# A two-layer hybrid decoder on one core: z's tiles in the form of the conv tiles, weight splits shared out anew between engines, one product for the mask of a head pair

## Chip, cores and metric

The kernel runs on one core of one Trainium2 chip. The metric is the device time of the program in microseconds (us). PE is TensorE's matmul stream, PEld its weight loads, DVE is VectorE, ACT is ScalarE, POOL is GpSimd, SP is SyncE, which issues most DMA transfers here.

## What is computed

A trunk of two layers over 256 tokens of width 1024, all in float32. From the reference, cut:

```python
mix = W_out( sigmoid(g_att) * P_att(MoBA(x)) + sigmoid(g_ssm) * P_ssm(Mamba2SSD(x)) )
h   = LayerNorm(ALPHA * x + mix)
x   = LayerNorm(ALPHA * h + W_down(relu(W_up h)^2))
...
q, k, v, z, xbc, dt_raw, g_att, g_ssm = _split(x @ w_in, IN_SPLITS)   # 1024 x3, 2048, 4096, 32, 1024 x2
...
xbc = jax.nn.silu(causal_dwconv(xbc, conv_w, conv_b))                 # 4 taps; xs 2048, B 1024, C 1024
dt = jax.nn.softplus(dt_raw + dt_bias)
a = -jnp.exp(a_log)
xdt = xs * dt[..., None]                                              # 32 heads of 64
decay = jnp.where(causal, jnp.exp(a_cs[..., :, None] - a_cs[..., None, :]), 0.0)   # a_cs = cumsum(dt * a)
y = einsum((C B^T of the head's group) * decay, xdt) + xs * d_skip    # 8 groups of 4 heads
hf = y * jax.nn.silu(z)
hf = hf * lax.rsqrt(mean over each group of hf^2 + RMS_EPS) * ssm_norm_w
```

The chunk of the state-space part is the whole sequence, so there is no carried state. The attention has 16 heads of 64 and one block, so it is plain causal attention.

## The kernel before

**Products.** Every large product multiplies x by weights in float32. Both are split into two parts: a high part, rounded by a cast to the type fp32r, and a low part, the difference. Three products of parts are added: high x high, high weight x low x, low weight x high x. `X[2*L]` holds x as `[128, 8, 2, 256]`: for each of eight k blocks of 128 channels the 256 tokens of the high part, and beside them the 256 of the low part. `gemm_ct` (L440) makes a tile of 128 output channels by 256 tokens with 24 matmuls of 256 columns (L446 to L448). `gemm_ct2` (L450), which the conv tiles use, runs the high weight over both parts of x in one matmul of 512 columns (`both`, L460), and the low weight over the high part in one of 256 columns (`left`, L467). Its output takes 512 columns of PSUM, a whole bank; the right half is then added to the left (`take_right`, a copy on ACT, L474; `add_left`, an addition on DVE, L477).

**Weights.** The weights come in 185 halves for each layer, of 128 x 1024 numbers each, in the order of use. A half is loaded by a DMA on SP (`load_half`, L129), its high part `whi` is cast on ACT (`high_half`, L136), its low part `wlo` is subtracted on DVE, or on GpSimd where `aside(h)` says so (`low_half`, L144):

```python
    def aside(h):

        return 5 <= h < 37 and h % 2
...
    def need(L, h, s, early=None):
        low = s - LOW_AHEAD if early is None else early
        lows[low].append((L, h))
        highs[low - 2].append((L, h))
        loads[low - 2 - LOAD_AHEAD].append((L, h))
```

Half 4 holds dt, halves 5 to 36 the 32 conv tiles, 37 to 56 q, k and v, 57 to 72 the 16 tiles of z, 73 to 88 the two gates.

**The order.** It is written out by hand in slots, 370 for each layer; `B` is the layer's first slot. A slot holds a piece of TensorE's large products (four k blocks of a tile in conv and z), and what `at(slot, function)` puts there on any engine. For each slot the program issues, in this order, the high casts, the low subtractions, the steps, the loads, and the slot's matmuls. A half is loaded fourteen slots ahead of its first matmul, cast six and subtracted four slots ahead. Every engine works off its own instructions in program order and waits on semaphores for its inputs.

**Stages.** In layer 0, in us of the profiled execution: the first q tiles to 22, dt 22 to 25, conv 25 to 126, q, k and v 126 to 195, z 195 to 255, gates 255 to 309, attention projection 309 to 333, state-space projection 333 to 377, output projection 377 to 400, the MLP 400 to 570. Layer 1 follows in the same order. The state-space and attention work of DVE, ACT and small matmuls runs beside the conv stage's end, q, k, v, z, and the gates: four heads of a group g at a time, a pair p of heads in one tile `E[p]` of 128 x 2 x 384 (`ss_exp`, then `ss_mask`, L823, then `ss_y`, L834).

**Around the change.** dt's product is evacuated by ACT into `dtc` (L487), transposed on TensorE (L492), and `dt_softplus` (L503 to L522) makes dt from it on DVE: seventeen small steps that wait on each other, with one Exp on ACT inside, all issued at slot B+13. Ahead of them on DVE, in layer 0, stand the steps that reduce the rope angles (L302 to L322). Each conv tile has three taps on DVE (L583), which read PSUM, and one on ACT. `z` and the gates are evacuated by `act_evac` and `gate_evac`, which apply Silu and Sigmoid on ACT as they read PSUM. ACT applies one function table at a time; a change of table is a table load of its own. Powers of the norms are the only GpSimd work in z's stage (L354, at 128 x 8).

## Time and profile before

| | us |
|---|---|
| median of 3 runs (range) | 1156.51 (1156.08 to 1157.07) |
| profiled execution, its own time | 1155.81 |
| its span | 1153.7 |
| PE busy | 1137.2 |
| DVE busy | 887.5 |
| ACT busy | 672.0 |
| POOL busy | 133.4 |

The span is the stretch from the first to the last instruction that the profiler recorded; the time of the execution holds 2.1 us more. The busy times are of that one execution. The granted clock of TensorE shows 9 in all forty slices of the page, nine tenths or more of full speed throughout.

### The profile page before, as it was taken

The numbers are of one execution on the slowest core, as the hardware profiler recorded it, in microseconds if no ns is written. First come the engines' busy times: TensorE is split into PE (matmuls) and PEld (weight loads), VectorE is DVE, ScalarE is ACT, GpSimd is POOL, SyncE is SP. The second block draws the span as 40 slices with busy tenths as digits, with TensorE's granted clock in tenths as the row PEclk, the third lists the DMA queues.
The fourth block names the chain that finished last, engine by engine and source line by source line (L and its number), as shares of the span: only waits on it lengthen the run. The fifth ranks groups of instructions, "written<-read, shape, count | busy, mean of one in ns | idle before, by whom it ended". The sixth has DMA issues, their size and how long they took to land.

```text
span 1153.7 us, 16860 instructions
## 1 busy us (share of the span) xinstructions
PE 1137.2 (99%) x6282; PEld 958.5 (83%) x6282; DVE 887.5 (77%) x1619; ACT 672.0 (58%) x1016; POOL 133.4 (12%) x99
## 2 busy tenths in 40 slices
PE   8999999999999999999999999999999999999997
PEld 5788888997888888888888888888878888888885
DVE  5899987899965884665779999778998569566565
ACT  5677755888743353453457776568887353444441
POOL 3344000011110000000033420000110100000001
PEclk9999999999999999999999999999999999999999
DMA  8545565545477456557444556645446655556630
GB/s 304 213 163 181 172 186 165 174 138 192 148 256 267 169 167 203 183 171 270 156 152 167 167 179 190 193 147 165 139 156 199 222 216 206 186 192 199 213 135 36
DMA packets 61392, 211.65 MB, mean 183 GB/s; under 512 B 7008, under 2 KB 7360, under 8 KB 61312
## 3 DMA queue, kind: packets, MB, share of 16 engines
q1 hardware_dynamic: 59696, 205.88, 53.7%
q0 software_dynamic: 1472, 4.46, 1.4%
q8 instruction: 49, 0.80, 0.3%
q14 instruction: 31, 0.25, 0.1%
q10 hardware_dynamic: 144, 0.26, 0.1%
HBM read 209.45 MB, written 1.11 MB: 183 GB/s over the span
## 4 chain that ended last, share of the span: by engine, by line
PE 92%; DVE 4%; DMA 1%; ACT 1%; issue 1%; SPq 0%; POOL 0%; DVEq 0%; POOLq 0%; ACTq 0%
PE up L460 9%; PE acc_x L460 8%; PE acc_d L154 5%; PE acc_d L156 5%; PE acc_d L155 5%; PE up L467 5%; PE acc_x L467 4%; PE acc_z L446 3%; PE acc_z L447 3%; PE acc_z L448 3%; PE yp L834 2%; PE sp L722 1%; PE av L765 1%; DMA raw<-in_w_dram 1%; DVE wlo L144 1%; PE acc_sp01b L171 1%
## 5 line engine op out<-in xcount | busy, mean ns | idle before, releaser
L144 DVE TENSOR_TENSOR wlo<-raw,whi 128x1024 fp32r<-128x1024 f32 (+1 forms) x341 | 428.2, 1272 | 25.7 <-ACT whi L136 7.8
L136 ACT CAST whi<-raw 128x1024 fp32r<-128x1024 f32 (+1 forms) x373 | 380.2, 1044 | 46.8 <-DVE wlo L144 17.1
L460 PE MATMUL acc_x<-x,whi 128*128 128x512 f32 x512 | 132.7, 395 | 0.0
L460 PE MATMUL up<-x,whi 128*128 128x512 f32 x448 | 114.9, 392 | 0.0
L477 DVE TENSOR_TENSOR rl<-up,rl 128x256 f32<-128x256 f32 x56 | 23.8, 425 | 117.0 <-ACT rl L474 117.0
L474 ACT COPY rl<-up 128x256 f32<-128x256 f32 x56 | 20.9, 373 | 142.4 <-PE up L460 142.4
L460 PEld LDWEIGHTS acc_x<-x,whi 128*128 128x128 f32 x512 | 90.7, 189 | 15.0
L583 DVE SCALAR_TENSOR_TENSOR cv<-acc_x,pc,cv 128x253 f32<-128x253 f32 (+2 forms) x192 | 91.9, 479 | 4.5
L144 POOL TENSOR_TENSOR wlo<-raw,whi 128x1024 fp32r<-128x1024 f32 x32 | 80.1, 2504 | 124.0 <-ACT whi L136 93.2
L460 PEld LDWEIGHTS up<-x,whi 128*128 128x128 f32 x448 | 80.4, 189 | 14.0
L467 PEld LDWEIGHTS acc_x<-x,wlo 128*128 128x128 f32 x512 | 70.6, 190 | 8.1 <-DVE wlo L144 2.5
L467 PE MATMUL acc_x<-x,wlo 128*128 128x256 f32 x512 | 75.3, 285 | 2.1 <-DVE wlo L144 2.1
L354 POOL TENSOR_TENSOR rc<-rc,mhalf 128x8 f32<-128x8 f32 x16 | 28.9, 1803 | 406.1 <-DVE nm L742 238.3
L446 PE MATMUL acc_z<-x,whi 128*128 128x256 f32 x256 | 74.7, 292 | 0.0
L447 PE MATMUL acc_z<-x,whi 128*128 128x256 f32 x256 | 72.3, 283 | 0.0
L448 PE MATMUL acc_z<-x,wlo 128*128 128x256 f32 x256 | 72.3, 282 | 0.0
L467 PEld LDWEIGHTS up<-x,wlo 128*128 128x128 f32 x448 | 61.2, 190 | 4.4
L467 PE MATMUL up<-x,wlo 128*128 128x256 f32 x448 | 62.9, 283 | 0.0
L579 ACT ACTIVATE cv<-acc_x,pc 128x256 f32<-128x256 f32 x64 | 36.8, 574 | 44.3 <-DVE acc_x L477 44.3
L446 PEld LDWEIGHTS acc_z<-x,whi 128*128 128x128 f32 x256 | 48.7, 190 | 3.4 <-issue 3.3
L447 PEld LDWEIGHTS acc_z<-x,whi 128*128 128x128 f32 x256 | 48.9, 191 | 0.1
L448 PEld LDWEIGHTS acc_z<-x,wlo 128*128 128x128 f32 x256 | 48.8, 190 | 0.0
(964 smaller groups left out, 2405.1 us busy)
## 6 DMA issues: line engine op xcount, KB each, us to landing
raw<-in_w_dram SPq DMA_DIRECT2D x370, 512.0 KB, 4.1
pb<-csd SPq DMA_DIRECT2D x32, 256.0 KB, 3.9
ln<-in_lnp_dram POOLq DMA_DIRECT2D x16, 256.0 KB, 6.4
x_tok<-in_x_dram SPq DMA_DIRECT2D x1, 1024.0 KB, 8.5
xraw<-in_xT_dram SPq DMA_DIRECT2D x3, 256.0 KB, 7.3
...
```

Source lines behind the costliest of these rows:

```text
L136: nc.scalar.copy(out=W[key][:, c], in_=raws[key][:, c])
L144: eng.tensor_tensor(out=lo[:, c], in0=raw[:, c], in1=W[key][:, c].bitcast(F32), op=OP.subtract)
L154: nc.tensor.matmul(o, xh, wh, start=first, stop=False)
L155: nc.tensor.matmul(o, xh, wl, start=False, stop=False)
L156: nc.tensor.matmul(o, xl, wh, start=False, stop=last)
L446: nc.tensor.matmul(o, a, xh[:, kk, :], start=(k == 0), stop=False)
L447: nc.tensor.matmul(o, a, xl[:, kk, :], start=False, stop=False)
L448: nc.tensor.matmul(o, b, xh[:, kk, :], start=False, stop=(k == KD - 1))
L460: nc.tensor.matmul(o, wh[:, (4 * half + i) * 128:(4 * half + i) * 128 + 128], x2[:, kk].rearrange("p j s -> p (j s)"), start=(k0 + i == 0) ...
L467: nc.tensor.matmul(o[:, 0:S], wl[:, (4 * half + i) * 128:(4 * half + i) * 128 + 128], x2[:, kk, 0, :], start=False, stop=False)
L579: nc.scalar.activation(c, o, AF.Identity, scale=pc[:, q + 3:q + 4], bias=pc[:, q + 4:q + 5])
L583: nc.vector.scalar_tensor_tensor(out=c[:, d:S], in0=o[:, 0:S - d], scalar=pc[:, q + j:q + j + 1], in1=c[:, d:S], op0=OP.mult, op1=OP.add)
```

## The change

- z uses `gemm_ct2`: 8 matmuls of 512 and 8 of 256 columns for a tile. Each of the 16 tiles of a layer has a bank of its own, a right copy on ACT and a left addition on DVE; Silu then works in SBUF on two or four tiles at once.
- In the conv stage GpSimd makes the low part of the halves that 3 does not divide (21 a layer instead of 16). In z's stage it makes the low parts of the odd halves 57 to 71 and, new, the high casts of the even halves 58 to 72.
- The mask of a head pair is one product of `E[p]` with the group's masked C B^T; the factor dt is taken out of it and multiplied into the turned xs by GpSimd (`xs_dt`, two products of 128 x 512 for each of four blocks).
- The gates are copied out of PSUM by ACT, and the four sigmoids of a layer run on SBUF tiles at slots 180 and 181, behind the last attention Exp. ACT's table loads fall from 42 to 34.
- Both Exp of an attention head pair stand in one slot, both normalisations in the next; the steps of the state-space norm move by a slot or some.

```diff
     def aside(h):

-        return 5 <= h < 37 and h % 2
+        return 5 <= h < 37 and h % 3 or 57 <= h < 73 and h % 2
+    CAST_ASIDE = range(58, 73, 2)
...
         for c in pieces(key, only):
-            nc.scalar.copy(out=W[key][:, c], in_=raws[key][:, c])
+            copy = nc.gpsimd.tensor_copy if h in CAST_ASIDE else nc.scalar.copy
+            copy(out=W[key][:, c], in_=raws[key][:, c])
...
+        def xs_dt(b, t):
+            x = xs_t[b][:, t, :].rearrange("p (h d) -> p h d", h=8)
+            nc.gpsimd.tensor_tensor(out=x, in0=x, in1=P["dt"][:, t, 8 * b:8 * b + 8].unsqueeze(2).to_broadcast(
+                [128, 8, 64]), op=OP.mult)
...
-                    at(res(r + 12 + j), xs_turn, b, j)
+                    e = res(r + 12 + j)
+                    at(e, xs_turn, b, j)
+                    at(e, xs_dt, b, j)
...
-            for j in range(2):
-                nc.scalar.activation(d[b][:, 2 * j:2 * j + 2, :].rearrange("p k s -> p (k s)"), banks[j]["o"], func)
-
-        for b in range(4):
-            banks = [ct_bank(B + 114, 57, 4 * b + 2 * j, 4 * b + 2 * j + 2, "z") for j in range(2)]
-            at(B + 114 + 8 * b + 8, act_evac, zs, b, banks, AF.Silu, "z")
+        def z_slot(i, half):
+            if half == 0:
+                zb[i] = new_acc(f"acc_z{L}_{i}")
+            gemm_ct2(zb[i], 57 + i, half, lambda k: (X[2 * L][2], k))
+
+        def z_right(i):
+            if i % 4 == 0:
+                zs[i // 4] = u_tile(f"z{L}{i // 4}", shape=(128, 4, S))
+            take_right(zs[i // 4][:, i % 4, :], zb[i])
+
+        def z_left(i):
+            add_left(zs[i // 4][:, i % 4, :], zb.pop(i))
+
+        def z_silu(b, r=slice(0, 4)):
+            nc.scalar.activation(zs[b][:, r, :], zs[b][:, r, :], AF.Silu)
+
+        for i in range(16):
+            base = B + 114 + 2 * i
+            need(L, 57 + i, base)
+            for half in range(2):
+                slots[base + half] = (z_slot, i, half)
+            at(base + 2, z_right, i)
+            at(base + 3, z_left, i)
+            if i in (1, 3):
+                at(base + 4, z_silu, 0, slice(i - 1, i + 1))
+            elif i % 4 == 3:
+                at(base + 6, z_silu, i // 4)
...
             for t in range(2):
-                nc.scalar.activation(d[n][:, t, :], f.tile[t], AF.Sigmoid)
+                nc.scalar.copy(out=d[n][:, t, :], in_=f.tile[t])
+
+        def gate_sigmoid(d, n):
+            nc.scalar.activation(d[n], d[n], AF.Sigmoid)
...
+                at(B + GATES + n, gate_sigmoid, d, n)
...
             for i in range(2):
-                at(s + 1 + i, at_exp, 2 * p + i)
-                at(s + 2 + i, at_norm, 2 * p + i)
+                at(s + 1, at_exp, 2 * p + i)
+            for i in range(2):
+                at(s + 2, at_norm, 2 * p + i)
...
         def ss_mask(p):
-            e, dt, cb = E[p], P["dt"], cbm[p // 2]
-            for i in range(2):
-                h = 2 * p + i
-                for t in range(2):
-                    r = slice(256 * t, 256 + 128 * t)
-                    nc.vector.scalar_tensor_tensor(out=e[:, i, r], in0=e[:, i, r], scalar=dt[:, t, h:h + 1],
-                                                   in1=cb[:, r], op0=OP.mult, op1=OP.mult)
+            e = E[p]
+            nc.vector.tensor_tensor(out=e, in0=e, in1=cbm[p // 2].unsqueeze(1).to_broadcast([128, 2, 384]),
+                                    op=OP.mult)
...
-            s = free = max(v + 2, B + 114 + 8 * (g // 2) + 10, free + 7)
-            for i, step in ((-1, ss_gate), (1, ss_square), (2, ss_add), (3, ss_sq_high), (5, ss_sq_low)):
+            s = free = max(v + 2, B + 114 + (4 * g + 8 if g < 2 else 8 * (g // 2) + 13), free + 7)
+            for i, step in ((-1, ss_gate), (1, ss_square), (2, ss_add), (5, ss_sq_high), (6, ss_sq_low)):
```

**GpSimd at the head of the conv stage.** In the order rows a tile's name carries its half and a running number: `wlo_8_336` is the low part of half 8. GpSimd's first subtractions of layer 0, before:

```order
L144 TENSOR_TENSOR wlo_5_239<-raw_5_135,whi_5_219 128x1024
L144 TENSOR_TENSOR wlo_7_304<-raw_7_159,whi_7_261 128x1024
L144 TENSOR_TENSOR wlo_9_388<-raw_9_223,whi_9_334 128x1024
L144 TENSOR_TENSOR wlo_11_448<-raw_11_269,whi_11_416 128x1024
L144 TENSOR_TENSOR wlo_13_514<-raw_13_341,whi_13_475 128x1024
L144 TENSOR_TENSOR wlo_15_575<-raw_15_424,whi_15_543 128x1024
L144 TENSOR_TENSOR wlo_17_634<-raw_17_483,whi_17_602 128x1024
```

and now:

```order
L150 TENSOR_TENSOR wlo_5_239<-raw_5_135,whi_5_219 128x1024
L150 TENSOR_TENSOR wlo_7_304<-raw_7_159,whi_7_261 128x1024
L150 TENSOR_TENSOR wlo_8_336<-raw_8_196,whi_8_302 128x1024
L150 TENSOR_TENSOR wlo_10_418<-raw_10_241,whi_10_386 128x1024
L150 TENSOR_TENSOR wlo_11_448<-raw_11_269,whi_11_416 128x1024
L150 TENSOR_TENSOR wlo_13_514<-raw_13_341,whi_13_475 128x1024
L150 TENSOR_TENSOR wlo_14_545<-raw_14_394,whi_14_512 128x1024
L150 TENSOR_TENSOR wlo_16_604<-raw_16_453,whi_16_573 128x1024
L150 TENSOR_TENSOR wlo_17_634<-raw_17_483,whi_17_602 128x1024
L607 TENSOR_TENSOR xs_640<-xs_640,dt_356 128x512 x2
```

Halves 8, 10, 14 and 16 have come to GpSimd, halves 9 and 15 have left it, and two products of xs by dt (L607) stand between its subtractions.

**DVE at the end of the softplus chain in layer 0** (`dw` and `dt` are tiles of the chain, `acc_x` conv accumulators, `cv` conv outputs). Before, the chain's last steps and what stood behind them:

```order
L515 SCALAR_TENSOR_TENSOR dw_357<-dw_357 128x64 x6
L517 SCALAR_TENSOR_TENSOR dw_357<-dw_357 128x64
L519 SCALAR_TENSOR_TENSOR dt_356<-dt_356,dw_357 128x64
L522 TENSOR_TENSOR adt_376<-dt_356,aneg_355 128x64
L477 TENSOR_TENSOR acc_x_1_343<-acc_x_1_343,xr_0_338 128x256
L583 SCALAR_TENSOR_TENSOR cv_0_390<-acc_x_0_312,pc_169,cv_0_390 128x253
L583 SCALAR_TENSOR_TENSOR cv_0_390<-acc_x_0_312,pc_169,cv_0_390 128x254
L583 SCALAR_TENSOR_TENSOR cv_0_390<-acc_x_0_312,pc_169,cv_0_390 128x255
L144 TENSOR_TENSOR wlo_10_418<-raw_10_241,whi_10_386 128x1024
```

and now:

```order
L521 SCALAR_TENSOR_TENSOR dw_357<-dw_357 128x64 x6
L523 SCALAR_TENSOR_TENSOR dw_357<-dw_357 128x64
L525 SCALAR_TENSOR_TENSOR dt_356<-dt_356,dw_357 128x64
L528 TENSOR_TENSOR adt_376<-dt_356,aneg_355 128x64
L150 TENSOR_TENSOR wlo_9_388<-raw_9_223,whi_9_334 128x1024
L483 TENSOR_TENSOR acc_x_1_343<-acc_x_1_343,xr_0_338 128x256
L589 SCALAR_TENSOR_TENSOR cv_0_390<-acc_x_0_312,pc_169,cv_0_390 128x253
L589 SCALAR_TENSOR_TENSOR cv_0_390<-acc_x_0_312,pc_169,cv_0_390 128x254
L589 SCALAR_TENSOR_TENSOR cv_0_390<-acc_x_0_312,pc_169,cv_0_390 128x255
```

Half 10's subtraction, five rows behind the chain, is gone to GpSimd; half 9's stands right behind the chain's last step. Half 8's, which stood two rows ahead of the chain, is gone too.

**GpSimd in z's stage of layer 0** (`rc` is the group mean in the state-space norm, raised to the power -1/2). Before, this is all that GpSimd had between the conv stage and its loads of the norm's parameters:

```order
L354 TENSOR_TENSOR rc_2519<-rc_2519,mhalf 128x8
L354 TENSOR_TENSOR rc_2701<-rc_2701,mhalf 128x8
L354 TENSOR_TENSOR rc_2878<-rc_2878,mhalf 128x8
L354 TENSOR_TENSOR rc_3036<-rc_3036,mhalf 128x8
L354 TENSOR_TENSOR rc_3163<-rc_3163,mhalf 128x8
L354 TENSOR_TENSOR rc_3288<-rc_3288,mhalf 128x8
L354 TENSOR_TENSOR rc_3395<-rc_3395,mhalf 128x8
L354 TENSOR_TENSOR rc_3568<-rc_3568,mhalf 128x8
```

and now, from half 64's cast to the second power:

```order
L142 CAST whi_64_2177<-raw_64_2035 128x1024
L150 TENSOR_TENSOR wlo_63_2179<-raw_63_2001,whi_63_2131 128x1024
L142 CAST whi_66_2267<-raw_66_2107 128x1024
L150 TENSOR_TENSOR wlo_65_2269<-raw_65_2063,whi_65_2207 128x1024
L142 CAST whi_68_2354<-raw_68_2185 128x1024
L150 TENSOR_TENSOR wlo_67_2356<-raw_67_2149,whi_67_2317 128x1024
L360 TENSOR_TENSOR rc_2377<-rc_2377,mhalf 128x8
L142 CAST whi_70_2444<-raw_70_2283 128x1024
L150 TENSOR_TENSOR wlo_69_2446<-raw_69_2215,whi_69_2395 128x1024
L142 CAST whi_72_2530<-raw_72_2361 128x1024
L150 TENSOR_TENSOR wlo_71_2532<-raw_71_2331,whi_71_2500 128x1024
L360 TENSOR_TENSOR rc_2607<-rc_2607,mhalf 128x8
```

Above these rows stand six more of the same two kinds (halves 57 to 62). The first power (`rc_2377`) stands behind the subtraction of half 67, and the second behind that of half 71.

## Rows read from the trace of the kernel before

Rows of a timeline give the start in us, the length in us, then engine, line, operation, output from inputs with their shapes, and how many instructions are run together in the row (the length then goes from the first start to the last end); brackets give the idle time ahead of the row and what ended it. Rows of groups give the number of instructions, busy us, mean ns of one, then the idle time ahead of them. A row of a stretch gives its ends and length, the busy time of PE, PEld, DVE, ACT and POOL with their instructions, the granted clock, the DMA share and GB/s.

**Rows 1.** The page: busy time of engines, and the chain that ended last.

```profile
PE 1137.2 (99%) x6282; PEld 958.5 (83%) x6282; DVE 887.5 (77%) x1619; ACT 672.0 (58%) x1016; POOL 133.4 (12%) x99
...
PE 92%; DVE 4%; DMA 1%; ACT 1%; issue 1%; SPq 0%; POOL 0%; DVEq 0%; POOLq 0%; ACTq 0%
```

**Rows 2.** TensorE's timeline, 235.7 to 239 us (z's stage).

```profile
235.73 0.28 PE L448 MATMUL acc_z<-x,wlo 128*128 128x256 f32 x1
...
237.53 0.28 PE L448 MATMUL acc_z<-x,wlo 128*128 128x256 f32 x1
237.74 1.52 PE L834 MATMUL yp<-ev,xs 128*64 128x256 f32 x16
```

**Rows 3.** TensorE's timeline, a tile of the conv stage.

```profile
72.99 2.00 PE L460 MATMUL acc_x<-x,whi 128*128 128x512 f32 x8
...
75.79 0.40 PE L460 MATMUL acc_x<-x,whi 128*128 128x512 f32 x1
```

**Rows 4.** TensorE's timeline, the first conv tiles of layer 0.

```profile
29.73 0.30 PE L492 MATMUL dtt<-ident,dtc 32*128 32x32 f32 x2 [0.65 <-ACT dtc L487]
...
37.97 1.11 PE L467 MATMUL acc_x<-x,wlo 128*128 128x256 f32 x8
...
43.02 0.74 PE L467 MATMUL acc_x<-x,wlo 128*128 128x256 f32 x4 [2.10 <-DVE wlo L144]
```

**Rows 5.** VectorE's timeline, 20 to 45 us.

```profile
23.85 2.40 DVE L304 TENSOR_SCALAR nrev<-ang 128x16 f32<-128x16 f32 x1
...
27.54 1.43 DVE L311 SCALAR_TENSOR_TENSOR ang<-nrev,ang 128x16 f32<-128x16 f32 x7
...
32.10 1.68 DVE L505 SCALAR_TENSOR_TENSOR dw<-dt 128x64 f32<-128x64 f32 x1
...
35.67 3.62 DVE L515 SCALAR_TENSOR_TENSOR dw<-dw 128x64 f32<-128x64 f32 x6
...
39.84 0.22 DVE L522 TENSOR_TENSOR adt<-dt,aneg 128x64 f32<-128x64 f32 x1
```

**Rows 6.** Line L515: ns minimum/median/maximum, first to last start.

```profile
L515 DVE SCALAR_TENSOR_TENSOR dw<-dw x12: 224/226/2324, 35.7 to 604.2; 128x64 f32<-128x64 f32 x12
```

**Rows 7.** GpSimd's timeline, the second subtraction of layer 0.

```profile
23.81 2.41 POOL L144 TENSOR_TENSOR wlo<-raw,whi 128x1024 fp32r<-128x1024 f32 x1 [0.16 <-DVE ang L302]
```

**Rows 8.** Groups from 60 to 125 us, VectorE's and GpSimd's.

```profile
L583 DVE SCALAR_TENSOR_TENSOR cv<-acc_x,pc,cv 128x253 f32<-128x253 f32 (+2 forms) x66 | 31.6, 478 | 1.6
L144 DVE TENSOR_TENSOR wlo<-raw,whi 128x1024 fp32r<-128x1024 f32 x13 | 24.8, 1909 | 0.0
L477 DVE TENSOR_TENSOR acc_x<-acc_x,xr 128x256 f32<-128x256 f32 x22 | 9.3, 424 | 2.0 <-ACT xr L474 2.0
...
L144 POOL TENSOR_TENSOR wlo<-raw,whi 128x1024 fp32r<-128x1024 f32 x9 | 22.4, 2494 | 30.4 <-ACT whi L136 18.5 <-issue 6.3 <-DVE cv L583 5.5
```

**Rows 9.** VectorE's timeline in z's stage, 232 to 240 us.

```profile
232.68 1.40 DVE L823 SCALAR_TENSOR_TENSOR ev<-ev,dt,cb 128x256 f32<-128x256 f32 x4
...
238.00 1.22 DVE L144 TENSOR_TENSOR wlo<-raw,whi 128x1024 fp32r<-128x1024 f32 x1
239.13 1.00 DVE L809 TENSOR_SCALAR ev<-pb,cst 128x256 f32<-128x256 f32 x4
```

**Rows 10.** Timeline of layer 1: softplus on VectorE, TensorE's use of half 9.

```profile
602.87 3.61 DVE L515 SCALAR_TENSOR_TENSOR dw<-dw 128x64 f32<-128x64 f32 x6
...
607.04 0.23 DVE L522 TENSOR_TENSOR adt<-dt,aneg 128x64 f32<-128x64 f32 x1
...
608.83 1.11 PE L467 MATMUL acc_x<-x,wlo 128*128 128x256 f32 x8
```

**Rows 11.** Groups of the whole span, of GpSimd and ScalarE.

```profile
L397 POOL TENSOR_TENSOR x_tok<-x_tok,ln 128x512 f32<-128x512 f32 x1 | 1.3, 1302 | 1.1 <-ACT x_tok L396 1.1
...
L587 ACT ACTIVATE cv<-cv 128x1024 f32<-128x1024 f32 x16 | 17.1, 1067 | 2.5 <-DVE cv L583 2.5
```

**Rows 12.** Busy time by stretch: z's stage of layer 0.

```profile
195.00:255.00 60.00, 60.00 (x517) 55.83 (x516) 52.34 (x147) 48.44 (x87) 3.44 (x2) 1.00 0.50 155
```

More of the change, by code (lines that the diff above doesn't have):

```diff
@@ L42 @@
 SS_AT = tuple(int(SS0 + SS_STRIDE * (2 * g + 1)) + 6 for g in range(8))
+GATES = 180
 AT_S = (98, 111, 118, 125, 132, 138, 145, 152)
@@ L671, in plan_layer @@
                     at(res(base + 13 + late), qk_turn, which, c, 1)
-        def ct_bank(base, h0, c0, c1, name):
-            g = {}
-            def slot(c, half):
-                if c == c0 and half == 0:
-                    g["o"] = new_acc(f"acc_{name}{L}_{c}")
-                gemm_ct(g["o"][:, (c - c0) * S:(c - c0) * S + S], h0 + c, half)
-            for c in range(c0, c1):
-                need(L, h0 + c, base + 2 * c)
-                for half in range(2):
-                    slots[base + 2 * c + half] = (slot, c, half)
-            return g
-        zs, ga, gs = {}, {}, {}
-        def act_evac(d, b, banks, func, name):
-            d[b] = u_tile(f"{name}{L}{b}", shape=(128, 4, S))
-            for j in range(2):
-                nc.scalar.activation(d[b][:, 2 * j:2 * j + 2, :].rearrange("p k s -> p (k s)"), banks[j]["o"], func)
-        for b in range(4):
-            banks = [ct_bank(B + 114, 57, 4 * b + 2 * j, 4 * b + 2 * j + 2, "z") for j in range(2)]
-            at(B + 114 + 8 * b + 8, act_evac, zs, b, banks, AF.Silu, "z")
+        zs, ga, gs = {}, {}, {}
+        zb = {}
+        def z_slot(i, half):
[21 more added lines that the diff above has]
+                at(base + 6, z_silu, i // 4)
         def gate_evac(d, n, f, name):
@@ L921, in plan_layer @@
             at(s, ss_mean, g)
-            at(s + 2, ss_rstd, g)
-            at(s + 2, ss_scale, g)
-            at(s + 3, ss_high, g)
-            at(s + 5, ss_low, g)
+            at(s + 3, ss_rstd, g)
+            at(s + 3, ss_scale, g)
+            at(s + 4, ss_high, g)
+            at(s + 6, ss_low, g)
         for p in range(8):
```

## The prediction

> **What bounds the kernel now.** I read the page first, then TensorE's own timeline, then the engines that feed it. PE is busy for 1137 of 1153.7 us, and the chain of waits that ended last runs over PE for 92% of the span [rows 1]. Only two things change the time, then: the length of PE's own instruction stream, and the places where PE stands and waits for a weight half or an SSM tile.
>
> How tight the stream is shows in its starts. In z's stage the products of 256 columns start 0.120 us apart (fifteen steps from 235.73 to 237.53) [rows 2]. A conv tile, which already uses the form that z is to get, takes 2.80 us for eight products of 512 and eight of 256 columns (72.99 to 75.79) [rows 3].
>
> Behind the start of the kernel, PE's waits in front of the first conv tiles are the ones to look at: 0.65 us for `dtc`, and 2.10 us for the `wlo` of half 10 [rows 4]. That low half comes from DVE, and why it is late is seen on DVE. Small operations that elsewhere take 0.2 us took 2.40 us (L304) and 1.68 us (L505), and one of the six of L515 took 2.32, where their median is 0.23 [rows 5, 6]. Each of these stretches lies inside a GpSimd subtraction: L304 started at 23.85 and ended at 26.25, the subtraction ran from 23.81 to 26.22 [rows 5, 7]. The low halves that DVE makes itself suffer too. From 60 to 125 us thirteen of them took 1909 ns each; undisturbed in z's stage, one takes 1.22 us [rows 8, 9]. That is 9.0 us lost to nine GpSimd subtractions, 1.0 us for each [rows 8]. The taps (L583), with one operand in PSUM, stay at 478 ns [rows 8]. So a GpSimd pass over wide tiles holds up DVE operations that read SBUF alone, `tensor_scalar` included (L304), and not those that read PSUM.
>
> **z side by side.** A z tile has now 24 products of 0.120 us, 2.88 us; as a conv tile it takes 2.80 [rows 2, 3]. Thirty-two tiles save 2.6 us, all of it on PE. The saving is the fixed cost of a third product, some 10 ns for each k. The Trainium skill (TensorE: Matmul & The Clock Gate, Back-to-back issue gap) gives an isolated product N/2.4 + 2.5 ns; the rows have about 13 ns over N/2.4 at 256 columns, so the page would make the saving 0.6 us, and the measured rows decide.
>
> **The front of the conv stage, layer 0.** GpSimd now takes halves 5, 7, 8, 10, 11 where it took 5, 7, 9, 11, and DVE gets half 9, which stands behind the whole softplus chain (DVE's order rows). Two things follow.
> (a) Half 8 follows half 7 on GpSimd directly, from 26.3 to 28.7. DVE then wants half 6 and the seven small steps of L311, which now run at 27.54 [rows 5]. They end 2.4 us later, and with them sin, `dtc` behind it on ACT, and PE's transposes at 29.73 [rows 4]. Cost: 2.4.
> (b) The softplus chain ends at 40.06 with one block of 1.45 (L505) and one of 2.1 (L515) [rows 5, 6]. Now it starts 2.4 later. The block by half 9 goes; halves 10 and 11 both fall into the chain, since their ACT casts stand right behind the chain's Exp. It ends at 40.06 + 2.4 - 1.45 + 2.4 = 43.4, and half 9 is done at 44.6. PE wants it at 37.97 + 2.4 = 40.4 [rows 4], so it waits 4.2 where it now waits 2.1 to 2.2 at half 10. Cost: 2.0.
> **Layer 1.** The chain ends at 607.27 with one block [rows 10]; with a second, 609.7, and half 9 at 610.9. PE wants it at 608.83 [rows 10] and does not wait today. Cost: 2.1.
> Bounds of the front: 0 if DVE slips through between the two subtractions; about 9 if half 6 is late too and half 12 behind it.
>
> The rest of the conv stage gets easier for DVE: five subtractions fewer for each layer, 6 us. GpSimd does 21 x 2.49 + 8 x 1.30 = 63 us (the product of x and dt by the one GpSimd product of 512 columns [rows 8, 11]) in a stage of some 100, so it holds. I put this at nothing.
>
> **z's stage on DVE.** DVE is busy 52.3 of 60.0 us there [rows 12]. Eight subtractions leave, 1.13 from start to start (238.00 to 239.13) [rows 9]: -9.0. A mask of four steps, 1.40 [rows 9], becomes one product of 768 columns, 0.92 between 0.42 (256) and 1.22 (1024): five pairs, -2.4. Sixteen left additions come, 0.42 [rows 8] less the 0.09 by which neighbours overlap: +5.4. Together 46.3, in a stage that is now 58.7: room for 12.4 us of waiting. GpSimd, busy there today with two powers only (3.44 us) [rows 12], gets 16 passes for each layer: eight subtractions at 2.49 and eight casts, which no row shows. A cast reads as many elements as the product of two tiles of 512 columns, 1.30; bounds are 1.07 (ACT on 1024 columns) and 2.49 [rows 8, 11]. I take 1.3, so 1.9 for a mean pass. What does a pass cost DVE? At least nothing, at most its whole length. I take the measured 1.0: these passes are shorter than the conv ones, but more of DVE's work here reads SBUF alone. 16.0, and 1.0 for powers that queue behind passes while a DVE transpose waits for them, make 17.0; that is 4.6 over the room. The slack is what stands between the end of a mask (234.08) and PE's use (237.74), 3.7 [rows 2, 9]. PE loses 0.9 a layer, 1.8 in all. Bounds: 0 and 29 (below).
>
> **Edits at nothing.** The right copies and the Silu on ACT are paid for by eight casts that leave and four table loads fewer a layer. The four sigmoids at slots 180 and 181 are one block on ACT of about 4 x 1.07 and a table load, some 6 us [rows 11], on an engine that is busy for 58% of the span [rows 1]; if that cover failed, a `whi` of the attention projection would be late by up to that much. Both Exp of a head pair in one slot, both scalings in the next: the scaled tiles are read thirteen slots after the scores, some 18 us. Steps of the norm a slot later: the last group is read twelve slots later. PSUM: z takes 16 banks where it took 8; gate 0 wants the bank of tile 13 three slots after its addition, so a late DVE shows there first.
>
> **The sum.** The profiled run took 1155.8. -2.6 (z) +4.4 (front, layer 0) +2.1 (layer 1) +1.8 (z's stage) = 1161.5. The median of the runs is 0.7 higher: **1162**.
>
> **Rivals.**
> *Faster.* DVE's delays stay inside the slack. Half 10's wait vanishes as GpSimd makes it, DVE gets its small steps in between passes, and z's stage stays under 12.4 + 3.7 = 16.1 us of waiting, 1.0 us a pass: the very point from which it decides. 1155.8 - 2.6 - 2.2 = 1151.0, as median 1151.7. For it: today PE waits almost nowhere although DVE has hardly an idle moment in the conv stage (1.6 and 2.0 us before its groups from 60 to 125) [rows 8]. Against it: every small DVE step that fell into a pass in rows 5 waited its end out. 0.18.
> *Heavy z.* Each pass is met near its start: 16 x 1.9 + 1.0 - 16.1 = 15.3 a layer, 1190; at 1.3 a pass 5.7 a layer, 1172. For it: over half of DVE's work there reads SBUF alone. The Trainium skill (SBUF — State Buffer, Who interferes with whom) has the pair of ports of GpSimd as an exclusive lock, held for a whole instruction, also against `tensor_scalar` in two-port modes. Rows 5 and 6 agree as to L304; no row has GpSimd wide at work in z's stage. By that rule alone, each pass met in full, the sum would be the 1190, by the conv rows the 1162. 0.17.
> *Half of it.* The form of z saves nothing beyond noise, or one of the two fronts does not bite: 1153.5 to 1158.5. 0.15.
> *Forecast*, front and some z waiting: 1158.5 to 1168, 0.50.
>
> Two runs of this kernel differ by about 0.1%, so 0.2% (2.3 us) tells a change from none. Faster (under 1154.2): 0.18 and a little of the half case, 0.20. Same: 0.15. Slower (over 1158.8): 0.65. The range for 8 in 10 leaves out the lower half of the faster case and the far part of heavy z: 1152 to 1174.
>
> **What would show it.** Right: z tiles of 2.80 us; PE waiting near 30 us (about 3) and at half 9 in both layers (4 and 2); L521, the new L515, with two long steps; DVE subtractions and masks in z's stage over 1.3 and 1.0 us. Wrong: PE's wait at half 9 missing, or DVE in z's stage idle as often as now; then the front or the price of a pass is mis-sized. If GpSimd casts take nearer 2.5 us, the heavy case has come.

## The result and the profile after

The changed kernel takes 1164.77 us (median of 5 runs, 1164.33 to 1167.06), the kernel before in the same series 1157.07 (1156.08 to 1157.69): a ratio of 1.0071, 95% interval 1.006 to 1.0082. It is slower by 7.7 us; 1162 had been forecast.

The profiled executions took 1155.81 and 1164.53 us. Their spans, 1153.7 and 1162.8 us, differ by 9.1. Where that arises is seen from the first matmul of each stage in TensorE's timeline (us):

| first matmul of | before | after | later by |
|---|---|---|---|
| conv, layer 0 | 24.73 | 25.12 | 0.40 |
| the cumulative sums (`csp`, behind the tile of half 9) | 43.69 | 48.46 | 4.77 |
| k, layer 0 (conv is over) | 125.81 | 129.88 | 4.07 |
| z, layer 0 | 194.91 | 198.98 | 4.07 |
| the first gate | 255.02 | 260.30 | 5.28 |
| the second gate | 284.07 | 289.68 | 5.61 |
| conv, layer 1 | 595.42 | 601.04 | 5.62 |
| k, layer 1 | 693.60 | 701.46 | 7.87 |
| z, layer 1 | 761.76 | 769.62 | 7.87 |
| the second gate, layer 1 | 850.91 | 860.33 | 9.42 |

So there are four losses: 3.7 us in the conv stage of layer 0 and 2.25 in that of layer 1, and 1.54 and 1.55 between the first matmul of z and the second gate. Outside them nothing moved by more than 0.4 us.

The page of the changed kernel, sections 1 and 4 (busy time of engines, chain that ended last), to be read against [rows 1]:

```profile
PE 1139.7 (98%) x6026; PEld 945.2 (81%) x6026; DVE 896.3 (77%) x1529; ACT 662.2 (57%) x1026; POOL 241.5 (21%) x157
...
PE 81%; DVE 11%; ACT 4%; DMA 2%; issue 1%; SPq 0%; POOL 0%; DVEq 0%; ACTq 0%; POOLq 0%
```

DVE has ninety instructions fewer and is busy for 8.8 us more; its share of the chain went from 4% to 11%. GpSimd is busy for 108 us more and has no share of the chain; the rows and runs below show that it does its harm through DVE.

**The front, layer 0.** TensorE's timeline (as in [rows 4]):

```profile
30.16 0.74 PE L473 MATMUL acc_x<-x,wlo 128*128 128x256 f32 x4 [1.16 <-DVE wlo L150]
...
32.21 0.42 PE L498 MATMUL dtt<-ident,dtc 32*128 32x32 f32 x2 [1.31 <-ACT dtc L493]
...
33.58 3.61 PE L466 MATMUL acc_x<-x,whi 128*128 128x512 f32 x8
...
45.00 1.22 PE L473 MATMUL acc_x<-x,wlo 128*128 128x256 f32 x8 [1.62 <-DVE wlo L150]
```

PE now waits for half 6, for `dtc` and for half 9. What holds these up is seen on DVE (as in [rows 5]):

```profile
24.25 2.38 DVE L310 TENSOR_SCALAR nrev<-ang 128x16 f32<-128x16 f32 x1
26.66 2.32 DVE L312 TENSOR_SCALAR nrev<-nrev 128x16 f32<-128x16 f32 x1
28.90 1.21 DVE L150 TENSOR_TENSOR wlo<-raw,whi 128x1024 fp32r<-128x1024 f32 x1
...
36.76 2.38 DVE L518 TENSOR_TENSOR dw<-dw 128x64 f32<-128x64 f32 x1
39.17 2.29 DVE L519 TENSOR_SCALAR dw<-dw 128x64 f32<-128x64 f32 x1
...
43.58 0.23 DVE L528 TENSOR_TENSOR adt<-dt,aneg 128x64 f32<-128x64 f32 x1
43.72 1.22 DVE L150 TENSOR_TENSOR wlo<-raw,whi 128x1024 fp32r<-128x1024 f32 x1
```

and on GpSimd (as in [rows 7]; the subtractions of halves 5, 7, 8, then 10 and 11):

```profile
21.63 7.32 POOL L150 TENSOR_TENSOR wlo<-raw,whi 128x1024 fp32r<-128x1024 f32 x3 [16.60 <-ACT whi L142]
36.67 4.75 POOL L150 TENSOR_TENSOR wlo<-raw,whi 128x1024 fp32r<-128x1024 f32 x2 [7.72 <-ACT whi L142]
```

A pass here is one GpSimd instruction over a tile of 128 x 1024. Four steps of 16 or 64 columns take 2.3 to 2.4 us, each about the length of a pass (7.32 us for three). DVE gets one instruction in between two passes, and half 6 (28.90) starts as the third pass ends at 28.95. The softplus chain ends at 43.81 and half 9 is there at 44.94. Eight matmuls of 512 columns at 33.58 took 3.61 us, where eight take 2.00 in [rows 3]: that is the clock. TensorE's granted clock in stretches of three us (columns as in [rows 12]):

```profile
30.00:33.00 3.00, 1.52 (x8) 1.26 (x9) 1.85 (x12) 1.03 (x5) 0.00 (x0) 0.76 1.03 410
33.00:36.00 3.00, 3.00 (x10) 2.52 (x10) 1.21 (x6) 2.97 (x6) 0.00 (x0) 0.50 0.75 299
36.00:39.00 3.00, 3.00 (x13) 2.66 (x13) 2.93 (x3) 2.25 (x4) 2.33 (x1) 0.60 0.01 5
39.00:42.00 3.00, 3.00 (x18) 2.62 (x18) 2.88 (x4) 0.00 (x0) 2.42 (x2) 1.00 0.00 0
```

From the second of the two waits on it stood at 0.50, 1.2 instead of 2.4 GHz, and took 3 x (0.24 + 0.50 + 0.40) = 3.4 us of PE's time in these stretches.

**The front, layer 1.** PE's waits from 600 to 620 us, where there was none before:

```profile
PE acc_x L473 <- DVE wlo L150: 1.6, 1, 1.6
```

**z's stage.** The names in its rows: `ev` is the state-space tile that Exp and mask work on, `yp` its product on PE. `sq` holds the squares for the state-space norm, `sh` their high and low parts, `sqp` the mean that PE makes of these. `pe` holds the attention weights, `nm` their minima and sums. A tile in its new form (TensorE's timeline, as in [rows 2]), and the stretch of the stage (as in [rows 12]):

```profile
212.85 1.11 PE L473 MATMUL acc_z<-x,wlo 128*128 128x256 f32 x8
213.80 2.00 PE L466 MATMUL acc_z<-x,whi 128*128 128x512 f32 x8
215.64 0.63 PE L473 MATMUL acc_z<-x,wlo 128*128 128x256 f32 x4
```

```profile
199.00:260.00 61.00, 59.39 (x388) 48.27 (x387) 58.80 (x132) 45.84 (x94) 24.69 (x13) 1.00 0.48 147
```

A tile takes 0.95 + 1.84 = 2.79 us, 0.09 less than before. But the stage is no shorter, and DVE is busy for 58.8 of 61.0 us. PE's waits there (engine, line, waited for: us in total, times, longest):

```profile
PE sqp L892 <- DVE sh L885: 0.8, 1, 0.8
PE sqp L892 <- DVE nm L752: 0.6, 1, 0.6
```

Both stand in front of the mean of the state-space norm: once its input `sh` is late, once the PSUM bank that it needs, which holds attention scores until DVE's L752 has read them. A third wait, 0.3 us for the same reason as the second, stands in the first gate. The first is plain on GpSimd's and DVE's timelines: `sh`, a subtraction of 256 columns, came 0.13 us behind the start of a pass and took 2.62 us.

```profile
226.60 2.46 POOL L150 TENSOR_TENSOR wlo<-raw,whi 128x1024 fp32r<-128x1024 f32 x1 [6.10 <-ACT whi L142]
```

```profile
226.73 2.62 DVE L885 TENSOR_TENSOR sh<-sq,sh 128x256 fp32r<-128x256 f32 x1
```

### The profile page after: what moved, and what is told of

The parts are those of the page before. It is cut to its first block, busy times and chain, and to the rows that moved or that the text cites. A ratio compares the mean times of both kernels' runs of the same rounds, so it can differ in the third digit from the quotient of the medians.

```text
span 1162.8 us, 16389 instructions
## 1 busy us (share of the span) xinstructions
PE 1139.7 (98%) x6026; PEld 945.2 (81%) x6026; DVE 896.3 (77%) x1529; ACT 662.2 (57%) x1026; POOL 241.5 (21%) x157
## 4 chain that ended last, share of the span: by engine, by line
PE 81%; DVE 11%; ACT 4%; DMA 2%; issue 1%; SPq 0%; POOL 0%; DVEq 0%; ACTq 0%; POOLq 0%
PE up L466 9%; PE acc_x L466 8%; PE acc_d L160 5%; PE acc_d L162 5%; PE acc_d L161 5%; PE up L473 5%; PE acc_x L473 4%; DVE wlo L150 2%; PE yp L853 1%; DVE ev L832 1%; DMA raw<-in_w_dram 1%; PE acc_sp11b L177 1%; PE acc_sp01a L177 1%; PE acc_sp01b L177 1%; PE acc_sp11a L177 1%
## 5 line engine op out<-in xcount | busy, mean ns | idle before, releaser
L150 DVE TENSOR_TENSOR wlo<-raw,whi 128x1024 fp32r<-128x1024 f32 (+1 forms) x315 | 393.4, 1266 | 22.2 <-PE acc_sp10b L177 4.5
L142 ACT CAST whi<-raw 128x1024 fp32r<-128x1024 f32 (+1 forms) x357 | 364.7, 1044 | 49.2 <-DVE wlo L150 19.5
L150 POOL TENSOR_TENSOR wlo<-raw,whi 128x1024 fp32r<-128x1024 f32 x58 | 150.8, 2615 | 119.1 <-ACT whi L142 90.9
L466 PEld LDWEIGHTS acc_x<-x,whi 128*128 128x128 f32 x512 | 91.7, 191 | 15.3
L466 PE MATMUL acc_z<-x,whi 128*128 128x512 f32 x256 | 68.7, 399 | 0.0
L426 POOL DMA_DIRECT2D ln<-in_lnp_dram x16 | 8.8, 554 | 238.6 <-PE acc_d L162 223.8
L466 PEld LDWEIGHTS acc_z<-x,whi 128*128 128x128 f32 x256 | 44.7, 189 | 9.0 <-issue 1.3
L142 POOL CAST whi<-raw 128x1024 fp32r<-128x1024 f32 x16 | 20.1, 1257 | 137.2 <-PE acc_k01b L177 65.3
L832 DVE TENSOR_SCALAR ev<-pb,cst 128x256 f32<-128x256 f32 (+1 forms) x128 | 45.5, 417 | 0.0
L483 DVE TENSOR_TENSOR acc_x<-acc_x,xr 128x256 f32<-128x256 f32 x64 | 27.2, 425 | 21.7 <-ACT xr L480 21.7
```

The costliest lines, as they stand in the source:

```text
L142: copy(out=W[key][:, c], in_=raws[key][:, c])
L150: eng.tensor_tensor(out=lo[:, c], in0=raw[:, c], in1=W[key][:, c].bitcast(F32), op=OP.subtract)
L466: nc.tensor.matmul(o, wh[:, (4 * half + i) * 128:(4 * half + i) * 128 + 128], x2[:, kk].rearrange("p j s -> p (j s)"), start=(k0 + i == 0) ...
L483: nc.vector.tensor_tensor(out=out if to is None else to, in0=o[:, 0:S], in1=out, op=OP.add)
L832: nc.vector.tensor_scalar(out=e[:, i, 256 * t:256 + 128 * t], in0=pb[:, i, 128 * t:256], scalar1=cst[:, t, h:h + 1], scalar2=0.0, op0=OP.s ...
```

## The experiments

The theory: a GpSimd pass over wide tiles holds up the DVE operations that read SBUF alone, at the front of the conv stage (rope steps, softplus chain) and in z's stage. Its rivals: the conv stage suffers as a whole; z's new form or the moved norm steps cost by themselves; DVE has simply too much to do. Every run had its time taken beside the kernel before on the same chip, and the ratio is to that; from series to series the median of the kernel before moved between 1156.68 and 1157.14 us, so differences of a few tenths between runs show nothing.

**1. Old front.** Among halves 5 to 12 the pattern of before:

```diff
-        return 5 <= h < 37 and h % 3 or 57 <= h < 73 and h % 2
+        return 5 <= h < 13 and h % 2 or 13 <= h < 37 and h % 3 or 57 <= h < 73 and h % 2
```

> The changed kernel, but among halves 5 to 12 GpSimd makes 5, 7, 9, 11 as before; from 13 on all as changed. Theory (GpSimd's passes at half 8 and inside the softplus chain hold DVE up): the losses of 4.4 us (layer 0) and 2.2 us (layer 1) ahead of the conv tiles go, 1164.8 - 6.6 = 1158.2; waits of PE are again some 0.65 us for dtc and 2.1 for half 10 in layer 0, none at half 9 in layer 1, and the granted clock stays at 1.0 from 33 to 38 us. Rival (the conv stage as a whole suffers from five more passes and eight products of xs by dt): under 1.5 us change, above 1163.

1159.34 us, ratio 1.0021 (1.0012 to 1.003). The front is worth 5.4 of the 7.7 us, 1.2 less than expected. PE waits for `dtc` (0.94) and half 10 (2.10) about as before, and for no half 9 in layer 1. The rest of the conv stage, with its additional passes from half 13 on, loses nothing to speak of: from `csp` to the first k tile it takes 82.20 us, before 82.12.

**2. Nothing of z on GpSimd.**

```diff
-        return 5 <= h < 37 and h % 3 or 57 <= h < 73 and h % 2
+        return 5 <= h < 37 and h % 3
-    CAST_ASIDE = range(58, 73, 2)
+    CAST_ASIDE = ()
```

> The changed kernel, but in z's stage the eight subtractions are on DVE and the eight casts on ACT again (z still side by side). Theory (passes hold DVE up, and with it sh and pe): PE's waits for sh and pe in z's stage and the first gate (2.5 us a layer) go, and DVE, though it has eight subtractions more, is less busy there than 57.7 of 60 us: 1164.8 - 5.0 = 1159.8. Rival (the side by side form itself costs: sixteen additions, sixteen copies, twice the banks): z's stage keeps its waits, above 1163. Rival (norm steps a slot later): the same, above 1163.

1165.08 us, 1.0071 (1.0057 to 1.0084): a miss in the time. In the profile two things cancel. From z's first matmul to the second gate the run takes 90.04 us, 0.66 less than the changed kernel, in either layer; its front, which is the same program as that of the changed kernel, is longer by 1.6 us. There the clock fell a second time, behind a wait of 2.99 us for half 9 (TensorE's timeline, and two stretches of two us):

```profile
45.31 1.57 PE L473 MATMUL acc_x<-x,wlo 128*128 128x256 f32 x8 [2.99 <-DVE wlo L150]
```

```profile
46.00:48.00 2.00, 2.00 (x9) 1.71 (x8) 1.91 (x5) 2.00 (x5) 0.00 (x0) 0.50 0.00 0
48.00:50.00 2.00, 2.00 (x8) 1.62 (x7) 1.93 (x5) 1.97 (x4) 0.71 (x1) 0.66 0.00 0
```

This fall took 2 x (0.50 + 0.34) = 1.7 us of PE's time. So z's stage gained 1.3 us of the 5.0 that were expected, and this time alone can't show it; run 3 does. The price of the passes on DVE is real. In 61 us from the first matmul of z on, DVE is busy for 4.9 us less than in the changed kernel, and makes sixteen subtractions there instead of nine (the stretch in run 2, and the group in run 2, then in the changed kernel from 199 to 260 us):

```profile
201.00:262.00 61.00, 60.00 (x391) 48.71 (x390) 53.87 (x141) 52.03 (x100) 3.44 (x2) 1.00 0.48 156
```

```profile
L150 DVE TENSOR_TENSOR wlo<-raw,whi 128x1024 fp32r<-128x1024 f32 x16 | 19.5, 1217 | 0.0
```

```profile
L150 DVE TENSOR_TENSOR wlo<-raw,whi 128x1024 fp32r<-128x1024 f32 x9 | 10.9, 1215 | 0.0
...
L150 POOL TENSOR_TENSOR wlo<-raw,whi 128x1024 fp32r<-128x1024 f32 x6 | 15.5, 2584 | 21.3 <-ACT whi L142 21.3
L142 POOL CAST whi<-raw 128x1024 fp32r<-128x1024 f32 x5 | 5.9, 1189 | 0.1
```

So eleven passes had cost DVE about 4.9 + 7 x 1.13 = 12.8 us, 1.2 each. But ACT is busy for 6.2 us more (the eight casts are back on it), and another wait takes the place of those for `sh`: PE at `yp`, in front of it the mask on DVE, in front of that the state-space Exp on ACT. Three views, TensorE, DVE and ACT:

```profile
244.46 0.87 PE L853 MATMUL yp<-ev,xs 128*64 128x256 f32 x8 [0.73 <-DVE ev L842]
```

```profile
243.44 0.96 DVE L842 TENSOR_TENSOR ev<-ev,cb 128x768 f32<-128x768 f32 x1 [1.10 <-ACT ev L838]
```

```profile
238.34 1.28 ACT L705 ACT_TABLE_LOAD   x1
239.63 1.06 ACT L705 ACTIVATE z<-z 128x1024 f32<-128x1024 f32 x1
240.60 0.35 ACT L480 COPY z<-acc_z 128x256 f32<-128x256 f32 x1
240.85 0.41 ACT L881 CAST sh<-sq 128x256 fp32r<-128x256 f32 x1
241.27 1.28 ACT L838 ACT_TABLE_LOAD   x1
242.57 0.84 ACT L838 ACTIVATE ev<-ev 128x768 f32<-128x768 f32 x1
```

The Silu of z stands in the program between the attention's Exp and this Exp, in the same slot as the latter, and brings two table loads with it. Here is a new theory for z's stage: each of these two arrangements has one late chain, DVE's `sh` with the passes, ACT's Exp without.

**3. Both back** (edits 1 and 2 together).

> Both of the former together: GpSimd's halves 5 to 12 as before, nothing in z's stage but its powers; the rest of the change stays. Theory: the two losses add up, 1164.8 - 6.6 - 5.0 = 1153.2, faster than before by the saving of z's form, 2 to 3 us and the conv stage's 0.7. Rival (the two share a cause, or the subtractions that return to DVE in z's stage make waits of their own): not under 1156.

1158.3 us, 1.0011 (1.0002 to 1.002). Not 1153: the front's part adds up (6.8 us against run 2, whose front had been 1.6 us longer than that of the changed kernel), z's brings 1.0 us against run 1 (0.7 a layer by the starts of stages) where 5.0 had been expected, with the same wait at `yp` (0.7 us by PE's waits).

**4. The norm's steps back** to their old offsets.

```diff
-            for i, step in (..., (5, ss_sq_high), (6, ss_sq_low)):
+            for i, step in (..., (3, ss_sq_high), (5, ss_sq_low)):
...
-            at(s + 3, ss_rstd, g)
+            at(s + 2, ss_rstd, g)
```

(and scale, high and low part a slot earlier too.)

> The changed kernel, but the steps of the state-space norm behind the sum stand where they stood before (high part of the squares at 3, low part at 5, rest a slot earlier). Rival (PE waits for sh because its steps were moved a slot back): the two waits of 0.8 to 1.0 us a layer go, 1164.8 - 3.6 = 1161.2. Theory (a GpSimd pass holds up the subtraction that makes sh, or the stream ahead of it): DVE works through the same passes, one slot of slack more for PE takes off at most half of it: 1163 to 1165.

1170.63 us, 1.0118 (1.0104 to 1.0132), a miss for theory and rival: 5.9 us worse than the changed kernel. The waits for `sh` went, and PE waits instead at the scores (0.33 us in layer 0), at `yp` (0.16 and 0.34), at the attention product (0.44) and again at `sqp` (0.68). The later steps of the change pay for themselves. That the steps now stand ahead of masks and normalisations on a full DVE would explain it; it was not tested.

**5. Half 8 alone back to DVE.**

```diff
-        return 5 <= h < 37 and h % 3 or 57 <= h < 73 and h % 2
+        return 5 <= h < 37 and h != 8 and h % 3 or 57 <= h < 73 and h % 2
```

> The changed kernel, but half 8's low part is made by DVE again; halves 10 and 11 stay on GpSimd, half 9 on DVE. The prediction's two steps apart: step (a), half 8 behind half 7 on GpSimd makes the rope steps and half 6 late, goes (PE's waits for half 6 and dtc fall from 2.5 to 0.7 us in layer 0); step (b), two subtractions inside the softplus chain and half 9 behind it, stays (PE waits some 4 us for half 9 in layer 0 and 1.8 in layer 1). Sum: some 2.4 us under the changed kernel, 1162.4. Rival (half 8 is all of it): 1158.5 to 1159.5. Rival (half 9's lateness is all of it, the first waits are only shifted ahead): 1164 to 1165.

1163.9 us, 1.0064 (1.0051 to 1.0076): 0.9 under the changed kernel, not 2.4, and the two intervals overlap; the conv stage of layer 0 is 0.7 us shorter in the profile. The wait for half 6 goes and that for `dtc` falls to 0.81, but PE then stands 4.36 us at half 9, and the clock falls in that wait:

```profile
43.14 2.08 PE L473 MATMUL acc_x<-x,wlo 128*128 128x256 f32 x8 [4.36 <-DVE wlo L150]
```

```profile
42.00:44.00 2.00, 0.86 (x4) 0.86 (x5) 1.96 (x4) 0.53 (x2) 0.00 (x0) 0.65 0.00 0
44.00:46.00 2.00, 2.00 (x9) 1.81 (x9) 1.93 (x5) 2.00 (x6) 0.00 (x0) 0.50 0.00 0
```

Half 9 is there at 43.01 instead of 44.86 (start of the next row on DVE), 1.85 us earlier; 2 x (0.35 + 0.50) = 1.7 us of PE's time go to the clock. That is what the second rival said: the chain's end decides, and what PE waits ahead of it is mostly taken from the wait at half 9.

**6. The pattern alone, on the kernel before.**

```diff
-        return 5 <= h < 37 and h % 2
+        return 5 <= h < 37 and h % 3
```

> The kernel before with one edit: GpSimd takes the halves of the conv stage that 3 does not divide. Theory (this pattern alone makes the front of the conv stage late): the 5.4 us between the changed kernel and the one with the old front come on top of before, 1157.0 + 5.4 = 1162.4, at least 1161. Rival (the pattern hurts only together with xs_dt or the other edits): 1157 to 1159.

1163.64 us, 1.0059 (1.0047 to 1.0072). One line of the change, without `xs_dt` or any other edit, makes 6.9 us.

**7. Casts on GpSimd, subtractions on DVE** (old front; `CAST_ASIDE` as in the change, no subtraction of z on GpSimd).

> Old front (halves 5 to 12 as before), and in z's stage the eight casts on GpSimd, the eight subtractions on DVE. So far: with both on GpSimd 1159.3, with neither 1158.3. Theory (subtractions on GpSimd hold DVE up, casts on ACT hold the state-space Exp up and with it the mask; each arrangement so far has one of the two): the casts alone relieve ACT at a small price, both waits (sh 1.0, yp 0.9 us a layer) go: 1156.5. Rival (a cast holds DVE up as a subtraction does): 1158.5 to 1160.

1157.62 us, 1.0007 (0.9998 to 1.0016), between the two expectations. A cast takes 1281 ns on GpSimd and costs DVE little: in the 60.30 us from 195.50 on DVE is busy for 56.03 us, in the same stage of run 3 for 53.40 of 60.50, so six casts cost 2.6 us, 0.4 each. DVE's steps of 128 and 256 columns at L766 take 361 ns in the mean, where both kinds of pass made it 463 and none 319 (runs 7 and 2 and the changed kernel, groups of z's stage):

```profile
L142 POOL CAST whi<-raw 128x1024 fp32r<-128x1024 f32 x6 | 7.7, 1281 | 27.9 <-PE acc_z L473 10.9 <-PE acc_v01b L177 9.2 <-PE acc_z L466 7.8
```

```profile
L766 DVE TENSOR_SCALAR pe<-pe,nm 128x256 f32<-128x256 f32 (+1 forms) x19 | 6.1, 361 | 0.3
```

Against run 1 (1159.34) the subtractions on GpSimd cost 1.7 us; by the starts of stages it is 0.86 us a layer, 90.74 less 89.88. Against run 3 (1158.3) the casts there give 0.7, which is within the intervals (0.2 us a layer by the starts).

**8. The Silu a slot later** (old front, nothing of z on GpSimd), so that the state-space Exp stands ahead of it.

```diff
-                at(base + 6, z_silu, i // 4)
+                at(base + 7, z_silu, i // 4)
```

> Old front, nothing of z on GpSimd, and the Silu of z's tiles one slot later, so that in the one slot where they meet the state-space Exp comes ahead of it, without a change of table between the attention's Exp and it. Theory (the yp wait of 0.9 us a layer is the Exp behind two table loads and a Silu): it goes, 1158.3 - 1.8 = 1156.5. Rival (DVE is late anyway, the mask finds other work ahead): above 1157.8.

1156.5 us, 0.9996 (0.9987 to 1.0005): the 1.8 us that were expected. The wait at `yp` fell from 0.7 to 0.3 us, and z's first matmul to the second gate from 90.06 to 89.11. The new theory of z's stage holds for the arrangement without passes. In this execution PE's wait of 2.10 us for half 10, which the profile of before shows without a fall of the clock, is followed by one (three stretches of two us):

```profile
44.00:46.00 2.00, 2.00 (x10) 1.27 (x11) 1.93 (x6) 1.85 (x4) 0.00 (x0) 0.74 0.00 0
46.00:48.00 2.00, 2.00 (x8) 1.71 (x7) 1.93 (x4) 1.93 (x4) 1.95 (x1) 0.50 0.05 13
48.00:50.00 2.00, 2.00 (x12) 1.73 (x12) 2.00 (x3) 0.04 (x1) 2.00 (x2) 0.90 0.68 180
```

That is 2 x (0.26 + 0.50 + 0.10) = 1.7 us of PE's time.

**9 and 10. A quiet front**, with z's casts on GpSimd (9) and without (10, the first of the two expectations); Silu as in run 8.

```diff
-        return 5 <= h < 37 and h % 3 or 57 <= h < 73 and h % 2
+        return 13 <= h < 37 and h % 3
```

> The changed kernel with the Silu a slot later, nothing of z on GpSimd, and no GpSimd subtraction ahead of half 13, so that none can fall on the rope steps or the softplus chain. Theory (four passes held DVE up by 2.3, 2.4, 1.45 and 2.1 us in the profile of before; the four subtractions cost DVE 1.13 each instead): DVE is 3.7 us earlier at the chain's end, PE's waits of 0.65 and 2.1 us go, granted clock 1.0 from 40 to 50 us: 1156.5 - 2.7 = 1153.8, faster than before. Rival (a pass costs DVE no more than the subtraction that it saves; the chain is late because DVE has too much to do): PE waits at half 9, 10 or 12 as long as now or longer, 1156 or more.

> As the next one (no GpSimd subtraction ahead of half 13, later Silu), with z's eight casts on GpSimd and its subtractions on DVE. Theory (with the Silu a slot later ACT is no longer what the state-space Exp waits for; half of the yp wait is left): at most 0.9 us under the next, 1153.2. Rival (a cast costs DVE as much as it gives ACT): the same as the next, or above it.

Without casts 1152.21 us, 0.9957 (0.9945 to 0.9969); with them 1152.07, 0.9957 (0.9944 to 0.9969). Both beat the kernel before by 4.9 to 5.1 us; the casts make no difference that can be seen. DVE, which makes four subtractions more there than before the change, ends the chain at 35.60 instead of 40.06, and PE's waits from 20 to 60 us (run 10) are down to this; DVE's two rows below it are the chain's end and the next subtraction, both undisturbed:

```profile
PE acc_x L473 <- DVE wlo L150: 0.2, 1, 0.2
```

```profile
35.38 0.22 DVE L528 TENSOR_TENSOR adt<-dt,aneg 128x64 f32<-128x64 f32 x1
35.52 1.22 DVE L150 TENSOR_TENSOR wlo<-raw,whi 128x1024 fp32r<-128x1024 f32 x1
```

**11. z in its old form**, otherwise as run 8 (norm steps as before, too).

> The run with old front, later Silu and nothing of z on GpSimd (1156.5), but z in the form of before (three products of 256 columns, Silu out of PSUM, norm steps where they stood before). What is left of the change: the mask in one product, xs by dt on GpSimd, the sigmoids, both Exp in one slot, the pattern of halves from 13 on. Theory (the form saves PE 1.1 us a layer, as acc_z's starts showed, and gives back 0.46 at yp and 0.45 at sqp in each): 1156.5 + 0.4 = 1156.9, and above 1156.5 at least. Rival (the form loses by its copies and additions): under 1156.

1155.83 us, 0.999 (0.9981 to 0.9999). The time is the rival's, under 1156 and not above 1156.5, but run 8 had 0.9996 with an interval that overlaps: z's form, with the norm's steps that go with it, is worth nothing that these runs can tell, in either direction. By the starts, run 8 is 0.4 us ahead of this run at the first gate (59.73 us from z's first matmul, here 60.11) and 0.2 behind it at the second: PE waits 0.29 us at `yp` and 0.30 at `sqp`, and here at neither.

**12. The quiet front alone, on the kernel before.**

```diff
-        return 5 <= h < 37 and h % 2
+        return 13 <= h < 37 and h % 2
```

> The kernel before with one edit: GpSimd makes no low part ahead of half 13 (13 to 35, odd, as before), DVE makes 5, 7, 9 and 11. Theory (what the last two runs gained on the kernel before is the front alone, 4.3 us from 1156.5 to 1152.2; the rest of the change gives 0.3): 1157.1 - 2.75 (the two waits of PE that stand in the trace of before) and up to 1.5 more where the granted clock had fallen behind them: 1152.9 to 1154.4. Rival (the gain needs the other edits too, which take work off DVE): 1156 to 1157.

1152.67 us, 0.9963 (0.995 to 0.9977). One line in the opposite direction to the change, less work on GpSimd, gives 4.0 us; the rest of runs 9 and 10 adds no more than the interval. PE has no wait left in the conv stage of layer 0, which takes 97.53 us for 101.08; layer 1, which had no wait there, gained nothing. DVE makes more subtractions here than before, so that it had simply too much to do is ruled out for the front.

**Stage by stage.** The starts of TensorE's matmuls in the profiled executions set the two stages apart. The conv stage of layer 0 holds the front and, where it fell, the clock; z's stage depends on neither (before, 6 and 12 agree). In us; layer 1 agrees with the second column within 0.1:

| run | first conv matmul to first k | first z matmul to second gate |
|---|---|---|
| before | 101.08 | 89.16 |
| changed | 104.76 | 90.70 |
| 1 old front | 101.47 | 90.74 |
| 2 nothing of z on GpSimd | 106.39 | 90.04 |
| 3 both back | 101.89 | 90.06 |
| 4 norm steps back | 104.75 | 92.84 |
| 5 half 8 back | 104.08 | 90.69 |
| 6 before, new pattern | 104.70 | 89.16 |
| 7 old front, casts alone | 101.13 | 89.88 |
| 8 as 3, later Silu | 101.86 | 89.11 |
| 9 quiet, later Silu, casts | 97.70 | 88.99 |
| 10 quiet, later Silu | 97.78 | 89.16 |
| 11 as 8, old form of z | 101.15 | 88.92 |
| 12 before, quiet | 97.53 | 89.15 |

## Why the prediction was right, step by step

**Right in size.** The range and the sign held, and so did the two largest losses, with their mechanism.
- *Front, layer 0*: 4.4 forecast; 4.37 by the start of `csp` (4.77 less the 0.40 of the start), of which the rest of the conv stage gave back 0.7. Half 9 was forecast at 44.6 and came at 44.94. Runs 1, 6 and 12 show that the pattern of halves does it, alone and in either direction. Step (a) was worth less by itself than its 2.4: run 5 gained 0.9 at most. Its wait stands ahead of that for half 9 and is mostly taken from it. Half 6 was late too, which the prediction had only in its bound of 9; its wait was 1.16. The two long steps of the chain, looked for in L521, were L518 and L519; the six of L521 took 1.52 in all.
- *Front, layer 1*: 2.1 forecast, 2.25 measured.
- *Price of a pass*: 1.0 us of DVE's time taken, 1.2 measured in z's stage (run 2), where eleven of the sixteen passes fell, of a mean length of 1.95. As the rows of before had it, steps that read PSUM are not touched: the taps stayed at 479 ns on the page of the changed kernel. Not lengthened, against the signs that the prediction named, were DVE's subtractions (1215 ns) and masks (954 ns) in z's stage; the steps of the norm and of attention were (`sh` above, L766 below run 7). The Trainium skill (SBUF — State Buffer, Who interferes with whom) names both sides of this: a DVE operation with two SBUF inputs contends with a GpSimd operation that reads SBUF, one with at most one SBUF input and outside the two-port modes does not. The trace agrees as to the taps and as to L518, which has two inputs (2.38 us); L519, a `tensor_scalar` with one, was held up too (2.29 us), which by that page takes a two-port mode, and no row here shows the mode. That rule taken at full length for each pass is the prediction's 1190; the passes took 1.2 of 1.95 us in the mean, and the casts of run 7 only 0.4 of 1.28.

**Right by luck.** PE's loss to the passes was put at 0.9 us a layer, and the subtractions on GpSimd cost 0.86 (run 1 less run 7). The way there was another: "The slack is what stands between the end of a mask (234.08) and PE's use (237.74), 3.7". The mask was not the tightest consumer. PE waited for `sh` of the norm and for the bank that the scores held, both late on a DVE that was busy for 58.8 of 61.0 us.

**Wrong.** From z's first matmul to the second gate a layer was to be 0.4 us shorter, 1.3 saved by the form and 0.9 lost to waits. It was 1.54 longer, which makes some 4 us in two layers and more than the whole miss of the sum. Two terms failed.
- *The saving of z's form*, "2.6 us, all of it on PE". A tile takes 2.79 us for 2.88, as the rows promised. By an estimate from the 2.5 ns that the Trainium skill (TensorE: Matmul & The Clock Gate, Back-to-back issue gap) gives as the fixed part of an isolated product it would have been 0.02 less; the trace shows 0.09. Nothing of this saving is left at the second gate: without passes and with the Silu moved (run 8) the stretch takes 89.11 us, with the old form (run 11) 88.92. PE waits for `yp` and `sqp` instead.
- *"Edits at nothing"*, the Silu and the table loads on ACT. Fewer loads were counted, but a Silu with two of them came to stand in front of a state-space Exp. Runs 2 and 3 laid it open, run 8 removed it for 1.8 us. In the changed kernel PE shows no wait at `yp`; what the order costs there by itself was not run. With the casts on GpSimd and the subtractions on DVE it cost 0.9 us a layer (run 7 less run 9, whose fronts differ too, which runs 8 and 10 show to be nothing for this stretch). The order of ACT's instructions tells it: in slot 134 the Silu stands ahead of the Exp. The prediction counted loads, and not the places where they stand.

From run 11 to the changed kernel the 1.8 us of this stretch then come as 0.2 for the form, -0.1 for the casts, 0.9 for the Silu's place and 0.8 for the subtractions (runs 11, 8, 9, 7, changed); the other edits had given 0.2. Taken in another order the parts may differ.

Two sums of the prediction are slightly off, without weight for the rest: the far bound of z's stage is 2 x 15.3 = 30.6, not 29, and sixteen additions at 0.33 are 5.3.

**Not foreseen.** The granted clock fell in the front of layer 0 and took 3.4 us of PE's time there. It did so in a stretch at whose end PE had to wait for half 9 anyway: the wait there was 1.62 us instead of the forecast 4.2, so the sum was hardly worse. In run 2, with the same front, the first fall took 1.7 us and the wait at half 9 was 2.99; there the clock fell once more behind that wait, and the stage grew by 1.6 us.
